# S5 without GpSimd: angles counted in turns, complex products of three multiplications, all elementwise work on VectorE

## The chip, the core and the metric

The kernel runs on one core of a Trainium2 chip. The core has four compute engines that run side by side, each with a queue of its own that it works through in order: TensorE (PE in the profile, its weight loads PEld), VectorE (DVE), ScalarE (ACT) and GpSimd (POOL). SyncE (SP) issues most of the DMAs. Semaphores order the engines among each other. The metric is the device time of one execution in microseconds; lower is better.

## The reference, cut to what matters

A decoder trunk of two layers over 1024 positions of width 1024. The first layer has RWKV-7 time mixing, an S5 state space model and an attention over a memory, side by side between one input and one output projection; the second has Mamba-2, latent attention and memory attention. The change concerns the S5 branch: 64 groups with 64 complex states each, 16 channels in and out of each group, and a diagonal recurrence.

```python
dt = jnp.exp(log_dt)[:, None]
mag = jnp.exp(lam_re * dt)
ab_re, ab_im = mag * jnp.cos(lam_im * dt), mag * jnp.sin(lam_im * dt)
den = lam_re * lam_re + lam_im * lam_im
f_re = ((ab_re - 1.0) * lam_re + ab_im * lam_im) / den
f_im = (ab_im * lam_re - (ab_re - 1.0) * lam_im) / den
bb_re = f_re[..., None] * b_re - f_im[..., None] * b_im
bb_im = f_re[..., None] * b_im + f_im[..., None] * b_re
...
# s_t = (ab_re + i ab_im) s_(t-1) + bb u_t, per group and state
y = jnp.einsum('blgn,gpn->blgp', s_re, c_re) - jnp.einsum('blgn,gpn->blgp', s_im, c_im)
...
y = jax.nn.gelu(y + d_skip * u)
return y * jax.nn.sigmoid(y @ glu_w + glu_b)
```

## The kernel before

Everything is computed in float32; a large product is made of three passes over operands split into a high and a low part (`split`, L402 to L405: a ScalarE copy `wh` or `yh`, a VectorE subtraction `wl` or `yl`).

The positions are cut into 128 blocks of eight steps, and the 64 groups into eight channel tiles `ct` of eight groups. With the powers 0 to 8 of the transition (`pr`, `pi`, made once in `s5_small`), a tile needs four steps, each a stream of its own:

- `s5_prep_x` turns the input matrix by the powers 0 to 7 (`rn`, a complex product of 512 elements a partition, real and imaginary part one after the other), transposes it on PE into `rt`, and makes the sine and cosine (`sn`, `cs`) of the angle of eight steps times the block number. For this ScalarE multiplies a row 0 to 127 by the angle of each group (L1338), and `reduce_angle` brings it into one period with six VectorE instructions (L1204 to L1208).
- `s5_prep_y` turns the output matrix by the powers 0 to 8 (`car`, `cai`, 576 elements a partition, six GpSimd products L1379 to L1384), multiplies it on PE with the input matrix into the kernel of one block (`ks`) and writes that to DRAM, to read it back as a Toeplitz matrix (`toe`).
- `s5_x` makes the input of each block on PE, turns it back by the block's angle (four VectorE products from PSUM, L1426 to L1429, two sums on GpSimd, L1432 and L1434), runs two scans over the blocks (L1433, L1435) and turns the result forward again (`hr`, `hi`: four products and two sums, two of the products on GpSimd, L1441 and L1443).
- `s5_y` multiplies `toe`, `car` and `cai` with the inputs and states on PE; `s5_tail` applies the GELU.

`s5_params` makes what all tiles share once, ahead of them: `bbr` on VectorE, `bbi` on GpSimd, the negated `ci` as `nci` on ScalarE. Most work tiles have one buffer, `car`, `cai`, `sn`, `cs`, `rt`, `hr`, `hi` two; where a buffer is taken again, its writer waits for the last reader.

A planner (`Flow`) writes down TensorE's order. Beside the S5 streams runs `dense`, at the lowest rank: the projections as a list of items of 24 matrix products a bank, which fill TensorE wherever no stream is ready. Their results are taken out of PSUM by ScalarE and VectorE, for a gate by L417 (`tanh`) and L418 (`ev`). The planner's waits (`yield`, with costs such as `S5A` and `S5B` in us, and `F.rel`, which gives a bank free after so many us) count only TensorE's columns. TensorE's instructions keep this order; the other engines' queues are ordered by the framework's scheduler. While S5 runs, the items are gates of the first layer, the memory keys and values of both layers and the first eight tiles of the output projection, whose operand `y` is loaded by DMAs that GpSimd issues (`y_load`, L1566); the memory attention of the first layer runs as well.

Of the kernel before, what the change touches and what calls it, by code (L numbers as in the profile page):

```python
# [10 lines left out]
F32 = mybir.dt.float32  # L11
F32R = mybir.dt.float32r
I32 = mybir.dt.int32
AF = mybir.ActivationFunctionType
A = mybir.AluOpType
# [4 lines left out]
P = 128  # L20
# [5 lines left out]
MAGIC = 12582912.0  # L26
TWO_PI = (6.28125, 0.0019350051879882812, 3.0199159819567e-07)
PI_IN = 3.1415925


COLS = [("norm_w0", 8), ("norm_w1", 8), ("mem_norm_w", 8), ("final_norm_w", 8),
# [233 lines left out]
class K:  # L265
# [941 lines left out]
            nc.vector.scalar_tensor_tensor(out, k, -cst, x if i == 0 else out, A.mult, A.add)  # L1207
        nc.vector.tensor_scalar(out, out, PI_IN, -PI_IN, A.min, A.max)  # L1208

    def sincos(self, s, c, r):  # L1210

        nc = self.nc
        nc.scalar.activation(s, r, AF.Sin)
        nc.scalar.activation(r, r, AF.Abs)
        nc.scalar.activation(c, r, AF.Sin, scale=-1.0, bias=self.halfpi)

    def s5_small(self, p):

        nc = self.nc
        sm = [p.tile([P, HT], F32, name=n, bufs=1) for n in ("ty", "sz")]  # L1220
        tmp = p.tile([P, 16, 32], F32, name="zi", bufs=1)
        self.s5d = self.dr.tile([P, 704], F32, name="s5d")
        q = self.s5_parts(*sm)
        free = iter(range(3, 16))
        t = lambda n: tmp[:, next(free)]
        lam = tmp[:, 0:3]
        nc.sync.dma_start(lam, self.I["s5_l"])
        lre, lim = lam[:, 0], lam[:, 1]
        dt, a1, th, r1, mag = t("dt"), t("a1"), t("th"), t("r1"), t("mag")
        tt, ts, stt = nc.vector.tensor_tensor, nc.vector.tensor_scalar, nc.vector.scalar_tensor_tensor  # L1230
        nc.scalar.activation(dt, lam[:, 2], AF.Exp)
        tt(a1, lre, dt, A.mult)
        tt(th, lim, dt, A.mult)
        nc.scalar.activation(mag, a1, AF.Exp)
        nc.scalar.activation(q["m8"], a1, AF.Exp, scale=8.0)
        k = t("k")
        self.reduce_angle(k, r1, th)
        ts(th, r1, 8.0, None, A.mult)
        self.reduce_angle(k, q["r8"], th)
        sn, cs = t("sn"), t("cs")  # L1240
        self.sincos(sn, cs, r1)
        pr, pi = q["pr"], q["pi"]
        nc.vector.memset(pr[:, :, 0], 1.0)
        nc.vector.memset(pi[:, :, 0], 0.0)
        tt(pr[:, :, 1], mag, cs, A.mult)
        tt(pi[:, :, 1], mag, sn, A.mult)
        ar, ai = pr[:, :, 1], pi[:, :, 1]
        u, v = t("pu"), t("pv")
        for e in range(2, 9):
            tt(u, pr[:, :, e - 1], ar, A.mult)  # L1250
            tt(v, pi[:, :, e - 1], ai, A.mult)
            tt(pr[:, :, e], u, v, A.subtract)
            tt(u, pr[:, :, e - 1], ai, A.mult)
            tt(v, pi[:, :, e - 1], ar, A.mult)
            tt(pi[:, :, e], u, v, A.add)

        nr, den = t("nr"), t("den")
        ts(nr, ar, 1.0, None, A.subtract)
        tt(den, lre, lre, A.mult)
        tt(u, lim, lim, A.mult)  # L1260
        tt(den, den, u, A.add)
        nc.vector.reciprocal(den, den)
        fr, fi = q["fr"], q["fi"]
        tt(u, nr, lre, A.mult)
        tt(v, ai, lim, A.mult)
        tt(fr, u, v, A.add)
        tt(fr, fr, den, A.mult)
        tt(u, ai, lre, A.mult)
        tt(v, nr, lim, A.mult)
        tt(fi, u, v, A.subtract)  # L1270
        tt(fi, fi, den, A.mult)
        nc.sync.dma_start(self.s5d[:, 0:416], sm[0][:, 0:416])
        nc.sync.dma_start(self.s5d[:, 416:704], sm[1][:, 0:288])
# [8 lines left out]
    def s5_params(self, p, tp):  # L1282
        nc = self.nc
        tt = nc.vector.tensor_tensor
        sm = p.tile([P, 704], F32, name="sm5")
        nc.scalar.dma_start(sm, self.s5d)
        q = self.s5_parts(sm[:, 0:416], sm[:, 416:704])
        fr, fi = q["fr"], q["fi"]
        bc = tp.tile([P, 2, 32, 16], F32, name="s5b")
        nc.scalar.dma_start(bc, self.I["s5_bc"][:, 0:2])  # L1290
        cc = p.tile([P, 2, 32, 16], F32, name="s5c")
        nc.scalar.dma_start(cc, self.I["s5_bc"][:, 2:4])
        q["cr"], q["ci"] = cc[:, 0], cc[:, 1]
        q["nci"] = p.tile([P, 32, 16], F32, name="nci")
        nc.scalar.mul(q["nci"], q["ci"], -1.0)

        b16 = lambda ap: ap.unsqueeze(2).broadcast_to([P, 32, 16])

        br = p.tile([P, 33, 16], F32, name="bbr")
        bi = p.tile([P, 33, 16], F32, name="bbi")  # L1300
        for o, x, y, op, eng in ((br, 0, 1, A.subtract, nc.vector), (bi, 1, 0, A.add, nc.gpsimd)):
            tmp = tp.tile([P, 32, 16], F32, name="bbt", bufs=2)
            eng.memset(o[:, 32], 0.0)
            eng.tensor_tensor(o[:, 0:32], bc[:, x], b16(fr), A.mult)
            eng.tensor_tensor(tmp, bc[:, y], b16(fi), A.mult)
            eng.tensor_tensor(o[:, 0:32], o[:, 0:32], tmp, op)
        q["br"], q["bi"] = br, bi
        io = tp.tile([P, P], I32, name="ioi")
        nc.gpsimd.iota(io, pattern=[[1, P]], base=0, channel_multiplier=0)
        iof = q["iota"] = p.tile([P, P], F32, name="iof")  # L1310
        nc.vector.tensor_copy(iof, io)
        nz = q["nz"] = p.tile([P, P], F32, name="nz")
        nc.vector.memset(nz, 1.0)
        nc.vector.memset(nz[:, 0:1], 0.0)
        kd = q["kd"] = self.dr.tile([8, 16, 8, 240], F32, name="kd")
        zt = tp.tile([P, 4, 112], F32, name="zt")
        nc.gpsimd.memset(zt, 0.0)
        for g in (0, 4):
            nc.scalar.dma_start(kd.rearrange("c q g f -> (c q) g f")[:, g:g + 4, 0:112], zt)

        dm = q["dm"] = p.tile([P, 16, 16], F32, name="dm")
        id16 = tp.tile([P, 16], F32, name="id16")
        nc.gpsimd.memset(id16, 0.0)
        for r in range(4):
            nc.vector.tensor_copy(id16[32 * r:32 * r + 16], self.ident[32 * r:32 * r + 16, 32 * r:32 * r + 16])
        o = COFF["s5_d"]
        nc.gpsimd.tensor_tensor(dm, id16.unsqueeze(1).broadcast_to([P, 16, 16]),
                                self.cols[:, o:o + 16].unsqueeze(2).broadcast_to([P, 16, 16]), A.mult)
        return q
    def s5_prep_x(self, q, ct, wk, st, free, wait):  # L1330
# [5 lines left out]
        ang = wk.tile([P, 4, P], F32, name="ang", bufs=1)  # L1336
        for g in range(4):
            nc.scalar.mul(ang[:, g], q["iota"], q["r8"][:, 4 * ct + g:4 * ct + g + 1])  # L1338
        self.reduce_angle(wk.tile([P, 4, P], F32, name="angk", bufs=1), ang, ang)

        e8 = lambda ap: ap[:, gs, 0:8].unsqueeze(3).broadcast_to([P, 4, 8, 16])
        b8 = lambda ap: ap[:, gs].unsqueeze(2).broadcast_to([P, 4, 8, 16])
        rs = []
        for x, y, op in (("br", "bi", A.subtract), ("bi", "br", A.add)):
            r = wk.tile([P, 4, 8, 16], F32, name="rn", bufs=2)
            t2 = wk.tile([P, 4, 8, 16], F32, name="rn2", bufs=1)
            tt(r, b8(q[x]), e8(q["pr"]), A.mult)
            tt(t2, b8(q[y]), e8(q["pi"]), A.mult)
            tt(r, r, t2, op)
            rs.append(r)  # L1350
        yield S5P
        yield free
# [2 lines left out]
        nc.sync.dma_start(u, self.ud[ct].rearrange("r (q g) b -> (r q) g b", q=16))  # L1355
        sn = st["sn"] = wk.tile([P, 4, P], F32, name="sn5", bufs=2)
        cs = st["cs"] = wk.tile([P, 4, P], F32, name="cs5", bufs=2)
        self.sincos(sn, cs, ang)
        rt = st["rt"] = wk.tile([P, 2, 4, P], F32, name="rt", bufs=2)
        for i, r in enumerate(rs):  # L1360
            yield ("g", 1)
# [6 lines left out]
    def s5_prep_y(self, q, ct, wk, st):  # L1368

        nc, F = self.nc, self.flow  # L1370
        gs = slice(4 * ct, 4 * ct + 4)
        pool_tt = nc.gpsimd.tensor_tensor

        e9 = lambda ap: ap[:, gs].unsqueeze(3).broadcast_to([P, 4, 9, 16])
        c9 = lambda ap: ap[:, gs].unsqueeze(2).broadcast_to([P, 4, 9, 16])
        tmp = wk.tile([P, 4, 9, 16], F32, name="cat", bufs=1)
        car = st["car"] = wk.tile([P, 4, 9, 16], F32, name="car", bufs=2)
        cai = st["cai"] = wk.tile([P, 4, 9, 16], F32, name="cai", bufs=2)
        pool_tt(car, c9(q["cr"]), e9(q["pr"]), A.mult)  # L1379
        pool_tt(tmp, c9(q["ci"]), e9(q["pi"]), A.mult)  # L1380
        pool_tt(car, car, tmp, A.subtract)
        pool_tt(cai, c9(q["cr"]), e9(q["pi"]), A.mult)
        pool_tt(tmp, c9(q["nci"]), e9(q["pr"]), A.mult)
        pool_tt(cai, tmp, cai, A.subtract)  # L1384

        ks = wk.tile([P, 2, P], F32, name="ks", bufs=1)
        yield S5Y
# [20 lines left out]
    def s5_x(self, q, ct, wk, st):  # L1408

        nc, F = self.nc, self.flow  # L1410
        pool_tt, tt = nc.gpsimd.tensor_tensor, nc.vector.tensor_tensor
        rt, u, sn, cs = (st[n] for n in ("rt", "u", "sn", "cs"))
        m8 = wk.tile([P, 4, P], F32, name="m85", bufs=1)
        for g in range(4):
# [14 lines left out]
        tt(t4, xr, sn, A.mult)  # L1429
        F.rel("g", 4.0)  # L1430
        F.rel("g", 4.0)
        pool_tt(t1, t1, t2, A.add)  # L1432
        nc.vector.tensor_tensor_scan(f2(t1), f2(m8), f2(t1), 0.0, A.mult, A.add)  # L1433
        pool_tt(t3, t3, t4, A.subtract)  # L1434
        nc.vector.tensor_tensor_scan(f2(t3), f2(m8), f2(t3), 0.0, A.mult, A.add)  # L1435
        hr = st["hr"] = wk.tile([P, 4, P + 1], F32, name="hr", bufs=2)
        hi = st["hi"] = wk.tile([P, 4, P + 1], F32, name="hi5", bufs=2)
        nc.gpsimd.memset(hr[:, :, 0:1], 0.0)
        nc.gpsimd.memset(hi[:, :, 0:1], 0.0)
        o = slice(1, P + 1)  # L1440
        pool_tt(t4, t1, sn, A.mult)  # L1441
        tt(hr[:, :, o], t1, cs, A.mult)
        pool_tt(t2, t3, sn, A.mult)  # L1443
        tt(hi[:, :, o], t3, cs, A.mult)
        tt(hi[:, :, o], hi[:, :, o], t4, A.add)
        tt(hr[:, :, o], hr[:, :, o], t2, A.subtract)
# [1023 lines left out]
```

## Time and profile before

| | |
|---|---|
| median of 3 runs | 2752.76 us (2747.67 to 2754.26) |
| profiled execution, its own time | 2737.01 us |
| its span, first to last instruction | 2735.0 us |
| PE busy | 2522.2 us (92%), 15058 matmuls |
| DVE busy | 1787.4 us (65%), 3382 instructions |
| ACT busy | 1250.9 us (46%), 2446 instructions |
| POOL busy | 797.9 us (29%), 1491 instructions |
| mean granted TensorE clock | 0.953 |

Busy is the time in which an engine runs at least one instruction. The granted clock is a share of full speed: 1.0 is 2.4 GHz, 0.5 is 1.2 GHz, and a mean between the two tells how long each was granted. "A <- B" in a list of waits reads: A's engine sat idle until B had ended.

### The profile page before, as it was taken

The numbers are of one execution on the slowest core, as the hardware profiler recorded it, in microseconds if no ns is written. First come the engines' busy times: TensorE is split into PE (matmuls) and PEld (weight loads), VectorE is DVE, ScalarE is ACT, GpSimd is POOL, SyncE is SP. The second block draws the span as 40 slices with busy tenths as digits, with TensorE's granted clock in tenths as the row PEclk, the third lists the DMA queues.
The fourth block names the chain that finished last, engine by engine and source line by source line (L and its number), as shares of the span: only waits on it lengthen the run. The fifth ranks groups of instructions, "written<-read, shape, count | busy, mean of one in ns | idle before, by whom it ended". The sixth has DMA issues, their size and how long they took to land. (4 is left out here: it accounts for less than half of the span.)

```text
span 2735.0 us, 42316 instructions
## 1 busy us (share of the span) xinstructions
PE 2522.2 (92%) x15058; PEld 2035.7 (74%) x15058; DVE 1787.4 (65%) x3382; ACT 1250.9 (46%) x2446; POOL 797.9 (29%) x1491
## 2 busy tenths in 40 slices
PE   7899999998999998787999998989899979999997
PEld 5777777786778776675678776767677768887786
DVE  8756676675656447888656357777733987777532
ACT  7443444343434334455534346435344646655443
POOL 3533553544345303354200111251311030000011
PEclk9989999999989899998999999999999999999999
DMA  4432233233232343465574564242445431114543
GB/s 149 130 100 89 89 95 98 90 90 90 91 98 65 80 135 134 122 187 151 188 245 145 159 191 127 69 120 74 109 149 176 144 113 55 57 51 137 172 133 102
DMA packets 263860, 328.27 MB, mean 120 GB/s; under 512 B 88017, under 2 KB 135249, under 8 KB 263137
## 3 DMA queue, kind: packets, MB, share of 16 engines
q1 hardware_dynamic: 260736, 319.39, 37.9%
q0 software_dynamic: 1280, 4.20, 0.5%
q8 instruction: 119, 1.95, 0.3%
q10 hardware_dynamic: 1632, 1.98, 0.3%
q14 instruction: 93, 0.75, 0.1%
HBM read 232.59 MB, written 92.90 MB: 119 GB/s over the span
## 5 line engine op out<-in xcount | busy, mean ns | idle before, releaser
L405 DVE TENSOR_TENSOR wl<-w,wh 128x512 fp32r<-128x512 f32 (+2 forms) x410 | 284.6, 698 | 279.4 <-ACT wh L404 273.2
L404 ACT CAST wh<-w 128x512 fp32r<-128x512 f32 (+2 forms) x410 | 241.8, 594 | 399.2 <-PE mm L179 253.0
L179 PE MATMUL mm<-xhi,wh 128*128 128x512 f32 x832 | 364.2, 438 | 22.6 <-DVE ev L418 15.9
L179 PE MATMUL mm<-xlo,wh 128*128 128x512 f32 x832 | 340.1, 409 | 4.8 <-DVE xlo L496 2.4
L179 PE MATMUL mm<-xhi,wl 128*128 128x512 f32 x832 | 338.6, 407 | 0.0
L179 PE MATMUL mm<-x1h,wh 128*128 128x512 f32 (+1 forms) x608 | 252.8, 416 | 23.9 <-ACT craw L1818 14.2
L710 POOL TENSOR_TENSOR titmp<-ai,ti 128x60 f32<-128x60 f32 (+24 forms) x496 | 157.2, 317 | 308.7 <-DMA ai<-d_in 271.4
L179 PE MATMUL mm<-x1h,wl 128*128 128x512 f32 (+1 forms) x608 | 242.4, 399 | 0.0
L179 PE MATMUL mm<-x1l,wh 128*128 128x512 f32 (+1 forms) x608 | 242.0, 398 | 0.0
L179 PEld LDWEIGHTS mm<-xhi,wh 128*128 128x128 f32 x832 | 162.6, 195 | 76.7 <-issue 20.4
L179 PEld LDWEIGHTS mm<-xhi,wl 128*128 128x128 f32 x832 | 162.8, 196 | 39.6
L179 PEld LDWEIGHTS mm<-xlo,wh 128*128 128x128 f32 x832 | 163.5, 196 | 36.8 <-DVE xlo L474 5.7
L712 POOL TENSOR_TENSOR ti<-ti,titmp 128x60 f32<-128x60 f32 (+24 forms) x496 | 166.3, 335 | 38.6
L179 PEld LDWEIGHTS mm<-x1h,wh 128*128 128x128 f32 (+1 forms) x608 | 117.0, 193 | 56.0 <-ACT craw L1818 16.5
L179 PEld LDWEIGHTS mm<-x1l,wh 128*128 128x128 f32 (+1 forms) x608 | 117.0, 192 | 27.7 <-issue 3.9
L179 PEld LDWEIGHTS mm<-x1h,wl 128*128 128x128 f32 (+1 forms) x608 | 116.4, 192 | 27.3 <-DVE wl L405 0.6
L179 PE MATMUL mm<-yb,wh 128*128 128x512 f32 x320 | 103.1, 403 | 4.5 <-ACT yb L404 4.0
L799 ACT ACTIVATE sn<-s0c,fin 64x64 f32<-64x64 f32 x128 | 44.1, 345 | 110.0 <-DVE s0c L827 58.1
L1669 POOL TENSOR_TENSOR sq<-sq,sqt 128x512 f32<-128x512 f32 x14 | 18.0, 1288 | 246.3 <-DMA w<-in_w_ev_out 161.3
L785 DVE TENSOR_TENSOR gb<-g,m 128x256 f32<-128x256 f32 x128 | 49.5, 417 | 56.1 <-PE g L179 55.7
L418 DVE SCALAR_TENSOR_TENSOR ev<-ev,mm 128x512 f32<-128x512 f32 x72 | 49.0, 681 | 43.8 <-ACT ev L417 43.5
L179 PEld LDWEIGHTS mm<-yb,wh 128*128 128x128 f32 x320 | 61.0, 191 | 21.0 <-ACT yb L404 4.5
(598 smaller groups left out, 6499.9 us busy)
## 6 DMA issues: line engine op xcount, KB each, us to landing
w<-in_w_ev_in SPq DMA_DIRECT2D x106, 256.0 KB
w<-in_w_od_in SPq DMA_DIRECT2D x82, 256.0 KB
w<-in_w_ev_out SPq DMA_DIRECT2D x64, 256.0 KB
w<-in_w_od_out SPq DMA_DIRECT2D x64, 256.0 KB
rd<-ev SPq DMA_DIRECT2D x50, 256.0 KB
spl<-yd SPq DMA_DIRECT2D x40, 256.0 KB
zod<-ev SPq DMA_DIRECT2D x36, 256.0 KB
ai<-d_in SPq DMA_DIRECT2D x16, 512.0 KB
```

The costliest lines, as they stand in the source:

```text
L179: return self._pe(self.nc.tensor.matmul(out, lhsT=lhsT, rhs=rhs, start=start, stop=stop, **kw), math.prod(rhs.shape[1:]), rhs.dtype)
L404: self.nc.scalar.copy(hi, src)
L405: self.nc.vector.tensor_tensor(lo, src, hi.bitcast(F32), A.subtract)
L418: nc.vector.scalar_tensor_tensor(g, g, 1.0, ps, A.add, A.mult)
L710: eng.tensor_tensor(tm, ai[:, s:s + 1, s + 1:32].broadcast_to([P, n, w]), ti[:, 0:n, s:s + 1].broadcast_to([P, n, w]), A.mult)
L712: eng.tensor_tensor(ti[:, 0:n, s + 1:32], ti[:, 0:n, s + 1:32], tm, A.subtract)
L785: nc.vector.tensor_tensor(gb[:, h], pgs[h], self.m2, A.mult)
L799: nc.scalar.mul(sg[hs], sc[hs, hs], g[hs])
L1669: nc.gpsimd.tensor_tensor(self.sq1, self.sq1, t, A.add)
```

## The change

All elementwise work of the S5 streams that GpSimd did goes to VectorE; GpSimd keeps memsets, the iota, a product of 256 elements in the setup and the issue of the y loads. The angle of a block is counted in turns: `r8` is divided by two pi once, a turn is taken off by adding and subtracting `MAGIC` (two instructions instead of six; the result has the opposite sign), and the factor two pi goes into the scale of the sine. Each complex product is made of three multiplications instead of four, one of them common to both parts, with sums (`bs`, `pp`, `pm`, `cp`) that are made once; `pm` takes the place of `pi`, and `cr` is negated in place of a copy of `ci`. Buffers and waits of the streams stay.

```diff
-    def sincos(self, s, c, r):
+    def sincos(self, s, c, r, unit=1.0):
-        nc.scalar.activation(s, r, AF.Sin)
+        nc.scalar.activation(s, r, AF.Sin, scale=unit)
         nc.scalar.activation(r, r, AF.Abs)
-        nc.scalar.activation(c, r, AF.Sin, scale=-1.0, bias=self.halfpi)
+        nc.scalar.activation(c, r, AF.Sin, scale=-abs(unit), bias=self.halfpi)
...
         self.reduce_angle(k, q["r8"], th)
+        ts(q["r8"], q["r8"], 1.0 / (2 * math.pi), None, A.mult)
...
-        q["nci"] = p.tile([P, 32, 16], F32, name="nci")
-        nc.scalar.mul(q["nci"], q["ci"], -1.0)
...
-        for o, x, y, op, eng in ((br, 0, 1, A.subtract, nc.vector), (bi, 1, 0, A.add, nc.gpsimd)):
+        for o, x, y, op, eng in ((br, 0, 1, A.subtract, nc.vector), (bi, 1, 0, A.add, nc.vector)):
...
+        for n, sh, x, y, op, eng in (("bs", 16, br[:, 0:32], bi[:, 0:32], A.add, nc.vector),
+                                     ("pp", 9, q["pr"], q["pi"], A.add, nc.vector),
+                                     ("pm", 9, q["pi"], q["pr"], A.subtract, nc.vector),
+                                     ("cp", 16, q["cr"], q["ci"], A.add, nc.vector)):
+            q[n] = q["pi"] if n == "pm" else p.tile([P, 32, sh], F32, name=n)
+            eng.tensor_tensor(q[n], x, y, op)
+        nc.scalar.mul(q["cr"], q["cr"], -1.0)
...
-        self.reduce_angle(wk.tile([P, 4, P], F32, name="angk", bufs=1), ang, ang)
+        k = wk.tile([P, 4, P], F32, name="angk", bufs=1)
+        nc.vector.tensor_scalar(k, ang, MAGIC, None, A.add)
+        nc.vector.scalar_tensor_tensor(ang, k, MAGIC, ang, A.subtract, A.subtract)
...
+        m = wk.tile([P, 4, 8, 16], F32, name="rn2", bufs=1)
+        tt(m, b8(q["bs"]), e8(q["pr"]), A.mult)
-        for x, y, op in (("br", "bi", A.subtract), ("bi", "br", A.add)):
+        for x, y, op in (("bi", "pp", A.subtract), ("br", "pm", A.add)):
             r = wk.tile([P, 4, 8, 16], F32, name="rn", bufs=2)
-            t2 = wk.tile([P, 4, 8, 16], F32, name="rn2", bufs=1)
-            tt(r, b8(q[x]), e8(q["pr"]), A.mult)
-            tt(t2, b8(q[y]), e8(q["pi"]), A.mult)
-            tt(r, r, t2, op)
+            tt(r, b8(q[x]), e8(q[y]), A.mult)
+            tt(r, m, r, op)
...
-        self.sincos(sn, cs, ang)
+        self.sincos(sn, cs, ang, -TURN)
...
-        pool_tt(car, c9(q["cr"]), e9(q["pr"]), A.mult)
-        pool_tt(tmp, c9(q["ci"]), e9(q["pi"]), A.mult)
-        pool_tt(car, car, tmp, A.subtract)
-        pool_tt(cai, c9(q["cr"]), e9(q["pi"]), A.mult)
-        pool_tt(tmp, c9(q["nci"]), e9(q["pr"]), A.mult)
-        pool_tt(cai, tmp, cai, A.subtract)
+        tt(tmp, c9(q["cp"]), e9(q["pr"]), A.mult)
+        tt(car, c9(q["ci"]), e9(q["pp"]), A.mult)
+        tt(car, tmp, car, A.subtract)
+        tt(cai, c9(q["cr"]), e9(q["pm"]), A.mult)
+        tt(cai, cai, tmp, A.subtract)
...
-        pool_tt(t1, t1, t2, A.add)
+        tt(t1, t1, t2, A.add)
...
-        pool_tt(t3, t3, t4, A.subtract)
+        tt(t3, t3, t4, A.subtract)
...
-        pool_tt(t4, t1, sn, A.mult)
+        tt(t4, t1, sn, A.mult)
...
-        pool_tt(t2, t3, sn, A.mult)
+        tt(t2, t3, sn, A.mult)
```

`TURN` is 2 x 3.1415925, `MAGIC` 12582912 (1.5 x 2^23: adding it to a small number rounds that to a whole one).

## Rows read from the trace of the kernel before

**Rows 1.** The page's busy tenths of TensorE in 40 equal slices of the span

```profile
PE   7899999998999998787999998989899979999997
```

**Rows 2.** Windows: stretch, its length, each engine's busy us (instructions), clock, DMA, GB/s

```profile
940.00:1040.00 100.00, 99.60 (x642) 79.77 (x641) 43.65 (x111) 32.82 (x68) 11.19 (x29) 1.00 0.39 118
1044.00:1322.00 278.00, 223.07 (x1512) 178.42 (x1512) 233.76 (x315) 143.39 (x292) 136.28 (x113) 0.88 0.50 150
1322.00:1422.00 100.00, 99.95 (x474) 78.18 (x473) 48.26 (x89) 43.10 (x79) 2.19 (x4) 1.00 0.75 244
```

**Rows 3.** Waits of TensorE, 1044 to 1332: us in total, times, longest

```profile
PE mm L179 <- DVE ev L418: 24.3, 5, 8.8
PE mm L179 <- DVE yl L405: 7.4, 2, 3.9
PE mm L179 <- ACT yh L404: 3.6, 1, 3.6
...
PE g L183 <- DVE rn L1349: 3.2, 1, 3.2
...
PE g L179 <- POOL cai L1384: 2.1, 1, 2.1
```

**Rows 4.** Timeline, 1054 to 1064: start, us, engine, line, what [idle before <- releaser]

```profile
1054.98 0.60 ACT L417 ACTIVATE ev<-mm 128x512 f32<-128x512 f32 x1 [1.67 <-PE mm L179]
...
1061.18 1.88 DVE L1347 TENSOR_TENSOR rn<-bbi,sm 128x512 f32<-128x512 f32 x1
...
1062.98 0.67 DVE L418 SCALAR_TENSOR_TENSOR ev<-ev,mm 128x512 f32<-128x512 f32 x1
...
1063.71 0.79 PE L179 MATMUL mm<-xhi,wh 128*128 128x512 f32 x1 [8.77 <-DVE ev L418]
```

**Rows 5.** Timeline of VectorE, 1106 to 1108

```profile
1106.31 0.68 DVE L1347 TENSOR_TENSOR rn<-bbi,sm 128x512 f32<-128x512 f32 x1
1106.91 0.42 DVE L1208 TENSOR_SCALAR ang<-ang 128x512 f32<-128x512 f32 x1
1107.24 0.68 DVE L405 TENSOR_TENSOR wl<-w,wh 128x512 fp32r<-128x512 f32 x1
```

**Rows 6.** Tiles `rn` and `m`: ns least/median/most, first and last start

```profile
L1349 DVE TENSOR_TENSOR rn<-rn,rn x16: 676/685/1896, 1064.6 to 1282.0; 128x512 f32<-128x512 f32 x16
...
L1433 DVE TENSOR_TENSOR_SCAN t<-m,t x8: 1210/1213/2310, 1095.3 to 1314.7; 128x512 f32<-128x512 f32 x8
```

**Rows 7.** Windows of 10 us inside the stage

```profile
1060.00:1070.00 10.00, 6.07 (x16) 4.56 (x16) 10.00 (x9) 0.62 (x1) 9.61 (x7) 0.53 0.23 83
1080.00:1090.00 10.00, 9.75 (x69) 7.77 (x68) 5.04 (x9) 6.41 (x10) 0.00 (x0) 1.00 0.39 120
```

**Rows 8.** VectorE groups, 1040 to 1330: count | busy us, mean | idle before

```profile
L405 DVE TENSOR_TENSOR wl<-w,wh 128x512 fp32r<-128x512 f32 x34 | 27.7, 818 | 15.4 <-ACT wh L404 15.3
L1207 DVE SCALAR_TENSOR_TENSOR ang<-angk,ang 128x512 f32<-128x512 f32 x24 | 22.4, 933 | 0.2
L1349 DVE TENSOR_TENSOR rn<-rn,rn 128x512 f32<-128x512 f32 x16 | 16.1, 1007 | 0.0
L1435 DVE TENSOR_TENSOR_SCAN t<-m,t 128x512 f32<-128x512 f32 x8 | 14.4, 1800 | 0.0
...
L1347 DVE TENSOR_TENSOR rn<-bbi,sm 128x512 f32<-128x512 f32 x8 | 10.3, 1288 | 0.0
...
L1444 DVE TENSOR_TENSOR hi<-t,cs 128x512 f32<-128x512 f32 x8 | 9.5, 1183 | 0.1
...
L1204 DVE TENSOR_SCALAR angk<-ang 128x512 f32<-128x512 f32 x8 | 9.0, 1119 | 3.1 <-ACT ang L1338 3.1
...
L1426 DVE TENSOR_TENSOR t<-g,cs 128x512 f32<-128x512 f32 x8 | 5.5, 684 | 3.1 <-PE g L179 3.1
...
L1305 DVE TENSOR_TENSOR bbt<-s5b,sm 128x512 f32<-128x512 f32 x1 | 1.6, 1555 | 0.0
```

**Rows 9.** Waits of GpSimd, 1040 to 1330

```profile
POOL car L1379 <- PE g L179: 7.7, 2, 6.7
```

More of the change, by code (lines that the diff above doesn't have):

```diff
@@ L28 @@
 PI_IN = 3.1415925
+TURN = 2 * PI_IN
 COLS = [("norm_w0", 8), ("norm_w1", 8), ("mem_norm_w", 8), ("final_norm_w", 8),
@@ L1371, in s5_prep_y @@
         gs = slice(4 * ct, 4 * ct + 4)
-        pool_tt = nc.gpsimd.tensor_tensor
+        tt = nc.vector.tensor_tensor
         e9 = lambda ap: ap[:, gs].unsqueeze(3).broadcast_to([P, 4, 9, 16])
@@ L1410, in s5_x @@
         nc, F = self.nc, self.flow
-        pool_tt, tt = nc.gpsimd.tensor_tensor, nc.vector.tensor_tensor
+        tt = nc.vector.tensor_tensor
         rt, u, sn, cs = (st[n] for n in ("rt", "u", "sn", "cs"))
```

## The prediction

> **What bounds the kernel now.** The page first: TensorE is busy nine tenths or more in most slices, and a row of weaker ones lies at the sixteenth to nineteenth, about 1025 to 1300 us [rows 1]. The windows show why that stretch stands out [rows 2]. Between 1044 and 1322 us, where S5's four streams run, PE is busy 223.07 of 278 us, at a mean granted clock of 0.88; in the 100 us before and the 100 us behind it PE is busy 99.60 and 99.95 at 1.00. So this stage holds 54.9 us of idle PE, and about 0.12 x 223 = 27 us that PE spends on top because it ran at the lower of its two levels (1.2 instead of 2.4 GHz); since idle and low stretches overlap, I take 24 us. Some 79 us is then the most that any change inside this stage can give. VectorE is busy 233.76 of the 278 us, GpSimd 136.28.
>
> The list of PE's waits says on what it waited [rows 3]: on the evacuation `ev` L418 24.3 us, on the splits `yl` and `yh` 11.0, on `rn` 3.2, on `cai` from GpSimd 2.1. L418 itself takes 0.67 us; it is late because of what stands before it in VectorE's queue. The timeline shows the longest case [rows 4]: ScalarE wrote its half of `ev` by 1055.6, VectorE got to L418 at 1062.98, and PE began again at 1063.71 after 8.77 us. In between stand S5 products such as L1347 with 1.88 us; the same line takes 0.68 us at 1106, where the next instruction starts 0.60 us behind it [rows 5].
>
> That lengthening is GpSimd's doing. `rn` L1349 takes 676 ns at the least and 1896 at the most, the scan L1433 1210 and 2310: same line, same shape [rows 6]. In 1080 to 1090, where GpSimd does nothing, nine VectorE instructions take 5.04 us together; in 1060 to 1070, GpSimd busy 9.61, nine take the whole 10 [rows 7]. And products with one input in PSUM keep their 684 ns (L1426), while L1444, with both inputs in SBUF, has a mean of 1183 [rows 8].
>
> **The change, part by part.** All durations are from the profiled execution: span 2735.0 us, its own time 2737.01, which is 15.8 us below the median of the timed runs, 2752.76. The difference worked out here is taken off that median.
>
> *What VectorE gets back.* For each SBUF-reading group in the stage: count x (mean - undisturbed value), which is 0.68 us for two-input instructions, 0.42 for `tensor_scalar` and 1.21 for the scan [rows 5, 6]. L405 `wl` 34 x 0.14 = 4.7; L1207 24 x 0.25 = 6.0; L1349 16 x 0.33 = 5.2; L1435 8 x 0.59 = 4.7; L1444 8 x 0.50 = 4.0; L1204 8 x 0.70 = 5.6 [rows 8]; the other thirteen groups of that view, down to L1305, give about 30 by the same subtraction. Together 60 us.
>
> *What leaves VectorE.* Per channel tile, eight in all: of the six instructions of the angle reduction two `tensor_scalar` (0.33 apart) and two `scalar_tensor_tensor` (0.60), and of the six `rn` products one (0.60) [rows 5]: 2.46 us, 20 us in all. The shorter angle chain also lets ScalarE's sines start earlier; I give that nothing.
>
> *What comes to VectorE.* Per tile five products of 576 elements for `car` and `cai`. VectorE has no such row. The lower bound is the 0.60 us between two starts at 512 elements [rows 5]; the upper one 1.45, the lengthened mean of L1347, 1.29, at 576 [rows 8]; I take 0.60 x 576/512 = 0.68, because L1347 has the same repeated operands and runs at the plain 0.68 where GpSimd rests. And four products of 512 (0.60): 5.8 us a tile, 46 us in all. Once: three products for `bbi`, one each for `bs` and `cp` (0.60 each) and two of 288 elements (0.35 each): 4 us. The negation on ScalarE takes the place of the one for `nci`, of the same shape; the factor inside the sine adds no instruction; the extra 32-column scaling falls in the stage before, where VectorE is busy 43.65 of 100 us [rows 2].
>
> *Sum for VectorE*: 233.8 - 60 - 20 + 46 + 4 = 204 us, 30 less than now. At the upper price the 40 products cost 31 us more, and VectorE is at 235, no better than now. GpSimd is left with memsets and the issues of the y loads.
>
> *What of it reaches PE.* VectorE still serves PE in a fixed order, and 204 us in a stage of 235 is 87%, as full as now (84%). I therefore don't let the idle time vanish. Wait by wait [rows 3]: L418, 24.3, comes down to 9, as the queue ahead of the longest one shrinks from some 14 us of lengthened work to 6, plus 4 of new setup products; `yl` and `yh`, 11.0, to 6, because they stand behind VectorE's lengthened work and behind ScalarE's own queue as well; `rn` 3.2 and `cai` 2.1 to 1 together; the rest, 14.3, waits for ScalarE, landings and issue, and loses a third: 9. That leaves 25 of 54.9. With fewer holes the low-clock stretches should shrink in about that proportion, 24 to 11. Gain: 30 + 13 = 43 us. Behind the stage PE is busy 99.95 of 100 [rows 2], so what it gains here moves the rest forward one for one. PE's own order is written by the planner, whose costs the change leaves alone.
>
> *A wait that moves.* `car` L1379 gets its buffer back only when PE has read the tile before last; GpSimd stood 7.7 us for this, harmlessly [rows 9]. On VectorE the same wait stands in front of evacuations, splits and `ks`, and PE waits for those. It costs nothing if the products are queued behind the release, 7.7 us otherwise; I take 2, as part of the 25.
>
> *A rule weighed.* The rows give 60 us as the price of GpSimd's company. The Trainium skill ("SBUF — State Buffer", section "Who interferes with whom") says that of a VectorE instruction with two SBUF inputs and a GpSimd instruction that reads SBUF, one blocks the other for its whole length. By that rule the price is an estimate of up to 0.84 x 136 = 114 us, if VectorE were always the one blocked, and VectorE ends at 150 us instead of 204. The 1896 ns of L1349 agree with a whole block; the mean of 1007 doesn't put every one on VectorE.
>
> **The rivals.** (a) *Chains bind, not VectorE's load.* PE and VectorE wait for each other through the recurrence, weights and landings, and a shorter queue only makes VectorE idle. For it: the 14.3 us of other waits. Against: `ev` heads the list. Then the longest `ev` wait loses 6 us, `rn` and `cai` 4, the clock gives 5: 15 us, 2738. (b) *VectorE's order gets in the way: slower.* The five products of `car` stand in one run before an evacuation, 3.4 us x 8 = 27 us, and the first of them waits for PE in every tile for 3.85 us, half of the 7.7 that GpSimd stood in two [rows 9], 31 us. 2753 - 43 + 27 + 31 = 2768. It decides where that wait passes (43 - 27)/8 = 2 us a tile. Against it: GpSimd waited in two tiles of eight. (c) *The lengthening isn't GpSimd's.* Then VectorE goes to 264 us, and at 84% load the stage grows to 314: 2789. Rows 6 to 8 speak against it. (d) *GpSimd holds VectorE up by more than the means show*: where VectorE stood still for GpSimd, what waited for its result stood as well. At 150 to 170 us VectorE is no longer near the bound; idle falls to 10, low clock to 4: 65 us, 2688.
>
> **How the numbers follow.** Forecast: 2753 - 43 = 2710, chance 0.55, own range 2695 to 2728. (d) 0.13, (a) 0.21, (b) 0.09, (c) 0.02. Runs of this kernel can tell about 0.3%, 8 us, from no change. Of (a) 0.09 and of (b) 0.01 fall within that bound; so faster 0.80, within 0.10, slower 0.10. The range, 2682 to 2742, takes in the forecast, (d) and the greater part of (a); left out are (b), (c) and the rest of (a).
>
> **What would show it.** In the profile after: L1349, L1444 and the scans at 0.68, 0.68 and 1.21 throughout the stage; VectorE busy near 204 us there, GpSimd under 10; the stage some 43 us shorter; PE's waits on L418 below 12 us and a granted clock above 0.93. It is wrong if VectorE's products stay lengthened; if the 576-element ones take 1 us or more; if L1379 waits for PE on VectorE and L418 waits behind it; or if PE's idle time only moves to weights, `yl` and landings.

## The result and the profile after

The changed kernel takes 2721.56 us (median of 4 runs, 2716.14 to 2726.14), where 2753.51 was measured beside it for the kernel before: a ratio of 0.9895, 95% interval [0.9872, 0.9918], 29 us less (23 to 35). A second series of the same kernel (e8 below) gave 0.9919 [0.9891, 0.9948], 22 us. The forecast was 2710. One of e4's six runs below, 2750.23 us, counts as slow and is left out of its ratio.

The page of the changed kernel, its profiled execution at 2720.39 us; the third line answers to [rows 1]:

```profile
span 2718.5 us, 42261 instructions
...
PE 2517.2 (93%) x15058; PEld 2032.4 (75%) x15058; DVE 1747.5 (64%) x3423; ACT 1248.3 (46%) x2443; POOL 670.2 (25%) x1407
...
PE   7899999998999989988999998988999979998997
```

For a comparison of all kernels below, the stage runs from the first product on VectorE in `s5_params` to the last matmul of `s5_y`. Its window in the kernel before (columns as in [rows 2]):

```profile
1048.60:1349.10 300.50, 245.57 (x1653) 195.44 (x1651) 244.45 (x341) 155.19 (x320) 135.44 (x107) 0.89 0.50 150
```

and in the changed kernel:

```profile
1049.90:1336.40 286.50, 252.44 (x1651) 201.06 (x1650) 206.51 (x380) 151.60 (x317) 7.81 (x24) 0.87 0.52 158
```

Length less PE's busy time is PE's idle time: 54.9 us before, 34.1 after. VectorE goes from 244.5 to 206.5 us with more instructions, GpSimd from 135.4 to 7.8. The granted clock is no better in this profile, 0.87 against 0.89: PE's own busy time for the same matmuls even rises by 7 us. The stretch that the prediction worked with, 1044 to 1322 in the kernel before [rows 2], stops short of this stage's end; its 1512 matmuls are done by about 1306 in the changed kernel:

```profile
1044.00:1306.00 262.00, 227.94 (x1506) 183.60 (x1504) 193.25 (x348) 138.70 (x285) 8.58 (x29) 0.86 0.52 159
```

VectorE's groups in the changed kernel, 1040 to 1330 (count | busy us, mean ns | idle before), to be held against [rows 8]; line numbers are up to 12 higher:

```profile
L406 DVE TENSOR_TENSOR wl<-w,wh 128x512 fp32r<-128x512 f32 x37 | 25.3, 684 | 18.0 <-ACT wh L405 18.0
...
L1361 DVE TENSOR_TENSOR rn<-rn,rn 128x512 f32<-128x512 f32 x16 | 10.8, 680 | 0.0
L1444 DVE TENSOR_TENSOR_SCAN t<-m,t 128x512 f32<-128x512 f32 x8 | 9.7, 1214 | 0.0
...
L1393 DVE TENSOR_TENSOR car<-cat,car 128x576 f32<-128x576 f32 x8 | 6.0, 751 | 0.1
...
L1455 DVE TENSOR_TENSOR hi<-t,cs 128x512 f32<-128x512 f32 x8 | 5.5, 681 | 0.0
```

No group is lengthened any more: `rn` 1007 to 680 ns, `hi` 1183 to 681, `wl`, which the change doesn't touch, 818 to 684. The products of 576 elements take 751.

PE's waits from 1044 to 1337 in the changed kernel, answering to [rows 3]:

```profile
PE g L180 <- ACT mpe L1138: 5.5, 1, 5.5
PE mm L180 <- DVE yl L406: 5.2, 2, 3.8
PE g L184 <- issue: 4.0, 1, 4.0
PE g L180 <- ACT mpt L1173: 3.3, 2, 2.7
PE g L180 <- DMA toe<-kd: 2.8, 1, 2.8
PE g L184 <- DVE mpe L1143: 2.6, 1, 2.6
PE mm L180 <- DVE ev L419: 2.0, 1, 2.0
PE mm L180 <- ACT ev L1045: 2.0, 2, 1.6
...
PE mm L180 <- ACT yh L405: 1.3, 1, 1.3
```

The evacuation `ev` (now L419), 24.3 us before, is down to 2.0. At the head stand waits on ScalarE and VectorE in the memory attention (`mpe`, `mpt`), which were small in the kernel before:

```profile
PE g L179 <- ACT mpe L1137: 0.8, 1, 0.8
PE g L179 <- ACT mpt L1172: 0.3, 1, 0.3
```

`mpe` is not at the head every time: in e8, the same program again, it is 1.1 us. The longest case of [rows 4] reads so in the timeline of the changed kernel:

```profile
1055.99 0.60 ACT L418 ACTIVATE ev<-mm 128x512 f32<-128x512 f32 x1 [0.89 <-PE mm L180]
...
1057.27 0.68 DVE L419 SCALAR_TENSOR_TENSOR ev<-ev,mm 128x512 f32<-128x512 f32 x1
...
1058.00 0.80 PE L180 MATMUL mm<-xhi,wh 128*128 128x512 f32 x1 [2.04 <-DVE ev L419]
```

VectorE gets to `ev` 0.7 us after ScalarE's half, not 7.4. The wait for `car` did move to VectorE, as in [rows 9], here from its list of waits:

```profile
DVE car L1392 <- PE g L180: 9.8, 2, 5.1
```

### The profile page after: what moved, and what is told of

The parts are those of the page before. It is cut to its first block, busy times and chain, and to the rows that moved or that the text cites. A ratio compares the mean times of both kernels' runs of the same rounds, so it can differ in the third digit from the quotient of the medians.

```text
span 2718.5 us, 42261 instructions
## 1 busy us (share of the span) xinstructions
PE 2517.2 (93%) x15058; PEld 2032.4 (75%) x15058; DVE 1747.5 (64%) x3423; ACT 1248.3 (46%) x2443; POOL 670.2 (25%) x1407
## 5 line engine op out<-in xcount | busy, mean ns | idle before, releaser
L786 DVE TENSOR_TENSOR gb<-g,m 128x256 f32<-128x256 f32 x128 | 49.4, 417 | 58.3 <-PE g L180 58.0
L180 PEld LDWEIGHTS mm<-yb,wh 128*128 128x128 f32 x320 | 61.4, 192 | 21.7 <-ACT yb L405 4.2
L419 DVE SCALAR_TENSOR_TENSOR ev<-ev,mm 128x512 f32<-128x512 f32 x72 | 49.0, 681 | 42.7 <-ACT ev L418 42.3
```

Of the source, the lines that this page charges most:

```text
L180: return self._pe(self.nc.tensor.matmul(out, lhsT=lhsT, rhs=rhs, start=start, stop=stop, **kw), math.prod(rhs.shape[1:]), rhs.dtype)
L419: nc.vector.scalar_tensor_tensor(g, g, 1.0, ps, A.add, A.mult)
L786: nc.vector.tensor_tensor(gb[:, h], pgs[h], self.m2, A.mult)
```

## The experiments

Two theories stood against each other. *Company*: GpSimd's products lengthen VectorE's, and the change gains by ending that. *Less work or a shorter chain*: the gain comes from fewer instructions, or from a recurrence that no longer passes through the slower GpSimd. Then came the question why only part of what VectorE got back reached PE. All ratios are against runs of the kernel before on the same chip; that kernel's median was 2745 to 2765 us from chip to chip, so ratios are compared and not times.

**e1: the arithmetic alone.**

```diff
-        tt = nc.vector.tensor_tensor       # s5_prep_y
+        tt = nc.gpsimd.tensor_tensor
-        tt(t1, t1, t2, A.add)              # and t3, t4, t2 of s5_x, and bbi
+        nc.gpsimd.tensor_tensor(t1, t1, t2, A.add)
```

> The changed kernel, with bbi, the five car/cai products and the four products and sums of s5_x back on GpSimd; angles in turns and three multiplications stay. Company (GpSimd's reads beside VectorE's lengthen VectorE's instructions, and the gain is that this ends): the gain goes, 2740 to 2753 us; L1361 rn and the scans are lengthened again, VectorE is busy about 215 us in the stage, GpSimd about 115. Less work (the gain is the 16 + 8 instructions fewer per pair of tiles): the gain stays, 2715 to 2727.

Ratio 0.9983 [0.9960, 1.0005]: the gain is gone. Its stage, and the spread of L1361 (least, median, most):

```profile
1053.40:1354.50 301.10, 250.29 (x1653) 198.86 (x1652) 226.38 (x305) 151.89 (x319) 121.96 (x99) 0.87 0.50 150
```

```profile
L1361 DVE TENSOR_TENSOR rn<-rn,rn x16: 675/682/1917, 1071.0 to 1283.2; 128x512 f32<-128x512 f32 x16
```

Fewer instructions on VectorE (226 us) beside 122 us of GpSimd leave PE 50.8 us idle, nearly as before. Less work is not the cause by itself. (It is ten instructions less on VectorE for a pair of tiles, four of the angle and one of `rn` in each, not the 16 + 8 of the expectation.)

**e2: the move alone.**

```diff
-        pool_tt = nc.gpsimd.tensor_tensor      # kernel before: s5_prep_y, s5_x, bbi
+        pool_tt = nc.vector.tensor_tensor
```

> The kernel before with only the move to VectorE; angles keep six instructions, complex products four multiplications. Company: VectorE is busy 233.8 - 60 + 8 x (6 x 0.68 + 4 x 0.60) + 2 = 228 us at undisturbed durations, about 24 more than in the changed kernel, and most of the gain is there: 2725 to 2740. Less work: no gain or a loss, 2753 to 2775, since VectorE has 10 more instructions per tile.

Ratio 0.9964 [0.9937, 0.9991], about 10 us. Its stage:

```profile
1059.10:1349.90 290.80, 243.80 (x1652) 194.66 (x1652) 229.36 (x424) 159.11 (x323) 7.88 (x24) 0.89 0.51 155
```

VectorE is at 229.4 us, PE idle for 47.0. The 228 of the expectation starts from 233.8, VectorE's time up to 1322 alone; from the stage's 244.5 the same sum gives 238, so more hold-up went than the 60 us reckoned with. With 0.65 us for a product of 576 elements (e5 below) and 0.60 for one of 512, what was added is 52 us, and the hold-up comes to an estimated 67. Company predicted that most of the gain would be there; between a third and a half is. The move alone gives 0.4%, the arithmetic alone 0.2%, which is not clear of nothing, both together 0.8 to 1.1%; that each helps the other is not shown, as the intervals are as wide as the difference. With GpSimd's products still there, 18 us less on VectorE took 4 us off PE's idle time (e1); without them 23 us less, from here to the changed kernel, took 13.

**e3: useless products on GpSimd beside the changed kernel.**

```diff
+        for _ in range(6):                     # s5_prep_y
+            nc.gpsimd.tensor_tensor(jk, c9(q["cr"])[:, :, 0:4], e9(q["pr"])[:, :, 0:4], A.mult)
+            nc.gpsimd.tensor_tensor(jk, c9(q["ci"])[:, :, 0:4], e9(q["pr"])[:, :, 0:4], A.mult)
...
+        for _ in range(4):                     # s5_x
+            nc.gpsimd.tensor_tensor(jk, cs[:, 0:2], sn[:, 0:2], A.mult)
+            nc.gpsimd.tensor_tensor(jk, sn[:, 2:4], cs[:, 2:4], A.add)
```

> The changed kernel, and GpSimd makes useless products whose result nobody reads: per tile 12 of 256 elements from the constants in s5_prep_y and 8 of 256 elements from cs and sn in s5_x, some 100 us of GpSimd time in the stage. Company: VectorE's two-input instructions are lengthened again, and the gain goes, 2740 to 2755. Chain (the gain is that the steps of the recurrence no longer pass through the slower GpSimd): the chain is as short as in the changed kernel, so 2716 to 2727. Less work: the same 2716 to 2727.

Ratio 0.9994 [0.9970, 1.0019]: products that nobody waits for take the whole gain away. The stage, L1361, and one of GpSimd's groups:

```profile
1061.90:1365.60 303.70, 252.46 (x1652) 201.65 (x1651) 250.52 (x380) 150.03 (x316) 172.28 (x184) 0.87 0.49 149
```

```profile
L1361 DVE TENSOR_TENSOR rn<-rn,rn x16: 676/682/1131, 1078.0 to 1294.9; 128x512 f32<-128x512 f32 x16
```

```profile
L1400 POOL TENSOR_TENSOR jk<-s5c,sm 128x256 f32<-128x256 f32 x48 | 42.4, 884 | 3.6
```

VectorE's same 380 instructions take 250.5 us instead of 206.5, and PE is idle for 51.2. The chain is as short as in the changed kernel, so the chain is not the cause. How much of the ratio is VectorE's hold-up alone is not separated: one wait of PE's is for `yh`, 1.3 us in the changed kernel and 10.6 here, and `yh` is made from the y loads, which GpSimd issues from the same queue as the useless products; whether these stood in its way is not shown.

```profile
PE mm L180 <- ACT yh L405: 10.6, 1, 10.6
```

The worst L1361 is 1131 ns here and 1917 in e1: the hold-up is smaller where GpSimd's product has 256 elements instead of 512 or 576.

**e4: useless memsets on GpSimd.**

```diff
+        for _ in range(24):                    # s5_prep_y; 16 in s5_x
+            nc.gpsimd.memset(jk, 0.0)
```

> The changed kernel, and GpSimd writes zeros into a tile nobody reads: per tile 24 memsets of 256 elements in s5_prep_y and 16 in s5_x, some 100 us of GpSimd time in the stage, none of it reading SBUF. If GpSimd's reads are what lengthens VectorE's two-input instructions (the Trainium skill, SBUF — State Buffer, section Who interferes with whom, names reads for these; no run here shows it so far): L1361 stays at 0.68 and the time at 2716 to 2730. If any company does it: lengthened, 2740 to 2755.

Ratio 0.9891 [0.9842, 0.9940], as the changed kernel. Stage, L1361 and one of the two groups of memsets:

```profile
1043.80:1317.40 273.60, 242.69 (x1651) 193.23 (x1649) 206.67 (x380) 151.01 (x317) 105.29 (x334) 0.92 0.54 165
```

```profile
L1361 DVE TENSOR_TENSOR rn<-rn,rn x16: 671/680/690, 1059.8 to 1244.8; 128x512 f32<-128x512 f32 x16
```

```profile
L1399 POOL MEMSET jk<- 128x256 f32 x192 | 60.8, 317 | 10.8
```

GpSimd is busy for 105 us in the stage and VectorE's two-input instructions aren't touched: L1361 takes 690 ns at the most, VectorE 206.7 us in all. For these it is what GpSimd reads that counts, not that it works. The Trainium skill ("SBUF — State Buffer", section "Who interferes with whom") says this of instructions with two SBUF inputs, and e3 and e4 agree. An instruction with one input in SBUF is touched a little by the memsets as well, 416 ns in the changed kernel and 490 here:

```profile
L1350 DVE TENSOR_SCALAR angk<-ang 128x512 f32<-128x512 f32 x8 | 3.9, 490 | 1.2 <-ACT ang L1347 1.2
```

**e8: the changed kernel again.** No edit.

> The changed kernel once more, for a second profile and a narrower interval. Clock by chance (the low-clock stretches of an execution don't follow from the stage's idle time): the time stays at 2716 to 2727, ratio 0.986 to 0.992, idle PE in the stage at 30 to 36 us as in the first profile, and the low-clock time of the stage, 72 us there, differs by 15 us or more. Clock by idleness: the same idle time, and 65 to 78 us at the low clock again.

Ratio 0.9919 [0.9891, 0.9948]. Its stage:

```profile
1072.10:1350.50 278.40, 245.54 (x1652) 196.46 (x1650) 206.63 (x380) 151.26 (x317) 7.89 (x24) 0.91 0.53 162
```

Idle 32.9 us, VectorE 206.6: as in the first profile to 1.2 us. Clock 0.91 against 0.87: twice (1 - clock) of the stage is spent at the lower level, 50 us here, 74 there. The stage is 8 us shorter with the same program, so idle time alone does not set the clock. A loose tie there is: 0.91 or 0.92 in the stages with 22 to 39 us idle (here, e4, and e5, e9 and e10 below), 0.87 to 0.89 in those with 47 to 55 us (before, e1, e2, e3, e12); the first profile (34.1 us, 0.87) and e6 (32.9 us, 0.88) lie outside it (e7 and e11 hold other matmuls in the stage). The timed runs, whose clock is known as a mean over the whole execution, lean the same way: 0.954 here (7 runs) against 0.952 in the 24 runs of the kernel before beside them, 0.959 against 0.952 in e4, 0.956 against 0.949 in e10. Through those 24 runs 0.001 of clock goes with 1.7 us, so an estimated 3 us of e8's 22 and 13 of e4's 30 came with the clock; the first of these is within the noise, and e11 below has 0.952 against 0.949 with less than half of the gain. What else sets the clock is open; the series ran on different chips, and chip and chance are not told apart.

**e5: 35 products less on VectorE.** `car` and `cai` are computed for the first tile alone and serve all eight.

```diff
+        if ct == 0:
+            ...
+            self.ca0 = car, cai
...
+        car, cai = st["car"], st["cai"] = self.ca0
```

> The changed kernel, but car and cai are computed for the first tile alone and used for all eight (seven tiles' output matrices are left out): 35 products less on VectorE, 0.67 us apart, 23 us, and the wait of car for PE (9.8 us in the changed kernel) is gone. Load (VectorE still binds the stage): VectorE falls from 206 to about 182 us and the time by 15 to 25 us, to about 2700. Waits moved (the rest of PE's idle time belongs to ScalarE and its queue, the memory attention and the landings): 2712 to 2724, nearly no change.

Ratio 0.9879 [0.9846, 0.9912], against e8's 0.9919 in the same series about 11 us, with intervals that overlap. Its stage:

```profile
1054.50:1318.30 263.80, 242.13 (x1652) 193.68 (x1651) 183.60 (x345) 152.60 (x318) 7.98 (x24) 0.91 0.57 171
```

23 us off VectorE take 11.2 to 12.4 us off PE's idle time (21.7): between the two theories of the expectation, half of the load counts. The wait of `car` for PE, 9.8 us on VectorE in the changed kernel, goes with the products here; e12 changes the load and leaves that wait's cause alone.

**e12: 40 products more on VectorE**, into a scratch tile.

```diff
+        for _ in range(5):                     # s5_prep_y, behind cai
+            tt(tmp, c9(q["cp"]), e9(q["pr"]), A.mult)
```

> The changed kernel, and VectorE repeats the product of 576 elements into the scratch tile cat five times per tile, 40 useless products 0.67 us apart: 27 us more in the stage, 206 to 233, without GpSimd. Exchange rate (about half a us of idle PE for each us on VectorE in this stage, as between before, changed and e5): idle 33 to 47 us, time 2733 to 2742 where the changed kernel has 2720 to 2727. Full rate (VectorE is the bound): 27 us, 2747 to 2755. Slack (VectorE has room): no change.

Ratio 0.9963 [0.9943, 0.9983]; times 2753 that is 2743, at the edge of what the exchange rate gives. Its stage:

```profile
1071.70:1368.80 297.10, 247.97 (x1653) 196.84 (x1652) 232.96 (x420) 150.48 (x316) 7.91 (x24) 0.88 0.51 152
```

26.4 us more on VectorE, idle 49.1, 15 to 16 us more. Here are VectorE's busy time and PE's idle time: 183.6 and 21.7 (e5), 206.5 and 34.1 (changed), 206.6 and 32.9 (e8), 229.4 and 47.0 (e2), 233.0 and 49.1 (e12), 244.5 and 54.9 (before). From e5 to e12 that is 27.4 over 49.4, 0.55 us of idle PE for one of VectorE, and the line meets e2 and the kernel before within 1 us. For VectorE's own work that is shown; for hold-up by GpSimd it is not, as the two other kernels with GpSimd's products lie off it: e1, 226.4 and 50.8, is 5 above, e3, 250.5 and 51.2, is 8 below. In e1, as in the kernel before, the chain passes through GpSimd and in e3 it doesn't, which would fit, but the chain was not tried by itself.

**e9: two buffers for `m8`.** In the changed kernel ScalarE stands for 15.2 us in front of `m` L1426, with `mpt` behind it:

```profile
ACT m L1426 <- DVE t L1446: 15.2, 5, 6.0
```

```diff
-        m8 = wk.tile([P, 4, P], F32, name="m85", bufs=1)
+        m8 = wk.tile([P, 4, P], F32, name="m85", bufs=2)
-        k = wk.tile([P, 4, P], F32, name="angk", bufs=1)
+        k = wk.tile([P, 4, P], F32, name="rn2", bufs=1)
```

> The changed kernel with two buffers for m8 (m85) instead of one; angk shares a buffer with rn2 to make room. In the changed kernel ScalarE stands in front of m L1426 for 15.2 us until VectorE's scan has read the old one, and behind it wait mpt and ks, for which PE waits. ScalarE's queue (the idle time that is left sits there): the wait is gone and PE's waits on mpt and mpe shrink, 2705 to 2716. Load of VectorE: no change, 2716 to 2727.

Ratio 0.9957 [0.9935, 0.9980], where the changed kernel has 0.9919 [0.9891, 0.9948] in the same series: no gain, and rather a loss. ScalarE's wait in this kernel, and the stage:

```profile
ACT m L1426 <- DVE t L1446: 8.7, 4, 2.5
```

```profile
1054.90:1336.40 281.50, 242.60 (x1653) 192.04 (x1651) 206.92 (x380) 151.56 (x317) 7.81 (x24) 0.91 0.53 161
```

The wait only halved, and PE is idle for 38.9 us. VectorE's order changed with the buffers, so this doesn't show what the wait alone is worth.

**e10: the scaling of the memory attention on ScalarE.**

```diff
-                nc.vector.tensor_scalar(pe[:, j, :], pe[:, j, :], sm[:, j:j + 1], None, A.mult)
+                nc.scalar.mul(pe[:, j, :], pe[:, j, :], sm[:, j:j + 1])     # first layer alone
```

> The changed kernel with the scaling of the first layer's memory attention (mpe, L1143: 32 instructions of 0.35 us in the stage on VectorE) on ScalarE. At the exchange rate: VectorE 206 to 196 us, 5 us less idle PE, 2715 to 2722, if ScalarE (139 of 262 us busy in the stage) has room. ScalarE's queue (what stands in front of mpt and ks): ScalarE gets 32 instructions of 0.47 us more, 15 us, and PE's waits on mpe and mpt grow, 2722 to 2735.

Ratio 0.9885 [0.9861, 0.9909], not to be told from the changed kernel's. Stage and two of PE's waits:

```profile
1067.70:1345.30 277.60, 243.67 (x1652) 194.54 (x1652) 197.75 (x348) 163.28 (x349) 7.89 (x24) 0.91 0.54 163
```

```profile
PE g L180 <- ACT mpt L1173: 4.3, 3, 2.6
PE mm L180 <- ACT ev L1045: 3.6, 2, 3.2
```

VectorE loses 9 us, ScalarE gains 12, idle stays at 33.9, where 0.55 for each us off VectorE would have taken 5 off. That fits a ScalarE queue which holds PE as well; it does not measure its share.

**e7, e11 and e6: the planner's delays.** Each changes TensorE's order.

```diff
-S5B = 30
+S5B = 20        # e7; 36 in e11
...
-NW0 = 6         # e6, with NW1 = 7 and NW2 = 2.5
+NW0 = 10        # NW1 = 12, NW2 = 5
```

> The changed kernel with the planner's delay between s5_x and s5_y (S5B) at 20 instead of 30 us, since the chain through s5_x no longer passes through GpSimd; TensorE's order changes. If this delay makes TensorE's order too slow for the shorter chain: the stage ends earlier and with less idle time, 2708 to 2718. If the order is bound elsewhere: 2716 to 2730, or slower where s5_y now comes too early.

> The changed kernel with the planner's S5B at 36 instead of 30 us; at 20 (e7) PE waited 21.0 us for the landing of toe, against 2.8 to 3.1 in the changed kernel. If s5_y is bound by toe: that wait goes to 0 and the time is 2716 to 2726. If the streams bind one another (a tile may only begin when s5_y of the tile before last is done): the stage gets longer, 2727 to 2745.

> The changed kernel with longer delays in the planner for the first layer's memory attention (10, 12 and 5 us instead of 6, 7 and 2.5 between loading, scores and products), so that TensorE's order asks for mpe and mpt later. In the changed kernel PE waits 5.5 us for mpe and 3.3 for mpt on ScalarE and 2.6 for mpe on VectorE, 11.4 us in all. Delays too short: these waits go, idle PE 34 to about 24 us, ratio 0.985 to 0.989. Streams bind one another (as where S5B was moved either way): the waits come up elsewhere, idle 34 or more, ratio 0.990 to 0.998.

Ratios 1.0020 [0.9992, 1.0049], 0.9962 [0.9944, 0.9980] and 0.9972 [0.9944, 1.0001]: all three lose most of the gain or all of it. In e7 PE waits for landings of `toe` and for `yh`:

```profile
PE g L180 <- DMA toe<-kd: 21.0, 4, 9.0
PE mm L180 <- ACT yh L405: 13.3, 2, 9.1
```

In e11 these two are gone and others stand in their place:

```profile
PE mm L180 <- ACT ev L1045: 8.8, 2, 8.3
PE g L180 <- ACT mpt L1173: 7.8, 1, 7.8
```

In e6 the waits for `mpt` go, and the idle time is 32.9 us as before, in other places. Each of these waits can be moved; in these three the idle time of the stage didn't fall (49.1 us in e7, 42.5 in e11). In e6 it didn't rise either, and most of the gain is gone all the same: the stage's idle time doesn't give the whole time. Its profile has 0.88 in the stage and its timed runs 0.950, against 0.951 in the kernel before; that the clock is the reason is not shown. No kernel here beats the changed one by more than the intervals.

## Why the prediction was right, and which term was mis-sized

**The mechanism held.** GpSimd's reads lengthen VectorE's two-input instructions; [rows 5 to 8] pointed to it, e3 and e4 showed it. Rival (c) is out.

**The parts of the sum for VectorE held; its gain was put too low.** The 204 us belong to the 1512 matmuls up to 1322, for which VectorE now needs 193 (1044 to 1306 above); over the whole stage it lost 38 us (244.5 to 206.5), not 30. The parts held: L1361, scans and `hi` at 0.68, 1.21 and 0.68; the 576-element products, taken at 0.68 from start to start, come to 0.65 (e5: 22.9 us less for 35 of them); GpSimd under 10. What was put too low is the hold-up, 60 us against an estimated 67 (e2). By the sum, two groups with one input in SBUF were not counted: L1142 `mpe`, 26 of 488 ns before and 348 now, and L1133 `mmx`, 14 of 324 and 159, are 6 us.

**What reaches PE was mis-sized.** The step took 30 us of idle time and 13 of clock for 30 us of VectorE. Measured were 21 to 22 us of idle time (54.9 to 34.1 and 32.9) for 38 us of VectorE, 0.55 for one. At that rate 30 us of VectorE would have given 16; that VectorE gave more than reckoned and PE took less partly cancels, and that is luck. Term by term: `ev` was forecast at 9 and came to 2.0, better than thought: VectorE gets to it 0.7 us after ScalarE's half; `yl` and `yh` came to 6.5, as forecast 6; but the remaining waits, forecast to lose a third of 14.3, rose to 25.6 (34.1 less 2.0 and 6.5; `rn` and `cai` are not in the list any more). So the term that failed is this rest: a PE that gets `ev` early comes to the next result before it is ready. That is what rival (a) had in mind, and e10 and e6, where idle time stays at 33.9 and 32.9, fit it; how much of the loss it explains is not shown. As a sum (a) is out: it gave `ev` 6 us less, and `ev` lost 22.

**The clock term is not borne out.** "In about that proportion" would have put the clock above 0.93. The two profiles of the changed kernel have 0.87 and 0.91 against 0.89, with idle times 1.2 us apart. The timed runs leave room for 3 to 13 us (e8), so how much of the gain beyond the 21 us of idle time is the clock's stays open. With both terms short, the stage is 14 us shorter in the first profile and 22 in e8, not 43.

**`car`'s wait** came, 9.8 us in two pieces against 7.7 on GpSimd, and cost little: `ev`, which it could have held up, has 2.0 us. Its point of decision, 2 us in every tile, was not reached, and rival (b) didn't occur.

**Rival (d)**, with VectorE at 150 to 170 us by a one-sided block, is out by VectorE's 193 in the stretch that these numbers belong to. GpSimd is held up as well: in e3 its L1400, always the same product, takes from 623 to 1432 ns.

## What to carry to other kernels

Before work is put on GpSimd as "free", look at the least and the most of VectorE's instructions of one shape; if they spread only where GpSimd reads SBUF, its work is paid for on VectorE, even on lines that have nothing to do with it. When VectorE serves a nearly full TensorE, don't count each us that it saves in full: here about half arrived. Ask which engine TensorE meets next. Don't credit the granted clock to a change on one profile: the same program had 0.87 and 0.91 in the same stage of two profiles.

## What the runs showed that was not expected

The stretch ahead of the stage has the same matmuls in the changed kernel, in e8 and in e4. Here are their windows from 0 to the stage's begin, one fence for each:

```profile
0.00:1049.90 1049.90, 977.79 (x7047) 777.01 (x7048) 665.04 (x1439) 439.04 (x901) 442.39 (x1152) 0.95 0.33 100
```

```profile
0.00:1072.10 1072.10, 1002.18 (x7047) 796.78 (x7048) 667.75 (x1440) 438.79 (x901) 438.51 (x1152) 0.93 0.33 98
```

```profile
0.00:1043.80 1043.80, 968.45 (x7047) 769.37 (x7048) 665.05 (x1439) 438.36 (x901) 444.93 (x1163) 0.96 0.34 101
```

VectorE's and ScalarE's times agree within 0.4%, PE's lie between 968 and 1002 us, with the mean clock at 0.96 to 0.93. So 28 us between two profiles, as much as the whole change gives, can come from the clock in a stretch that wasn't touched (e4 and e8 ran on different chips). The spans of the two first profiles, 2735.0 and 2718.5, differ by 16.5 us, little more than half of what the timed runs show, and are no measure of the change.
